# Two-layer streaming-encoder trunk: wide gate and up products and a chunk-row output for S5

## The chip, the cores and the metric

The kernel runs on one core of one Trainium2 chip, in one launch. The metric is the device time of one execution in microseconds, the median of the runs of a kernel. Lower is better.

## The reference, cut to what matters

x has 256 tokens of 1024 features. Each of the two layers computes, in fp32:

```python
h = rms_norm(x, ffn1_pre_g);  x = x + 0.5 * rms_norm(swiglu(h, w_gu, w_down), ffn1_post_g)
h = rms_norm(x, mix_pre_g);   x = x + rms_norm(hybrid_mixer(h, ...), mix_post_g)   # GLA, S5, FoX
h = rms_norm(x, xa_pre_g);    x = x + rms_norm(memory_cross_attention(h, ...), xa_post_g)
h = rms_norm(x, ffn2_pre_g);  x = x + 0.5 * rms_norm(swiglu(h, w_gu, w_down), ffn2_post_g)

def swiglu(h, w_gu, w_down):                      # w_gu 1024 x 5632, w_down 2816 x 1024
    gate, up = jnp.split(h @ w_gu, 2, axis=-1)
    return (jax.nn.silu(gate) * up) @ w_down
```

Inside the mixer, S5 is a grouped complex diagonal state-space model: y = Re(C x_t) + D u with x_t = A x_(t-1) + B u_t, then gelu(y), then y * sigmoid(y @ glu_w + b), then an up projection. The 256 tokens are worked as 64 chunks of 4 tokens.

## The kernel before, in words

**Products in three passes.** Every large operand is split into two fp32r parts: `split` (L232) casts it on ScalarE (`h`, L237) and subtracts on VectorE (`lo`, L241). `mm3` (L253) then issues three matmuls into one accumulator (L255): h·xh, h·xl, lo·xh. The activations x, transposed, stand in two tiles, `xth` (high) and `xtl` (low), 128 x 8 x 256 each, made by `xt` (L273).

**Weights.** `make_plan` lists all weights in the order in which they are used, in pieces of 128 x 1024. SP loads them into `wf` (5 buffers), `split_next` (L162) splits them into a ring `wh`, `wl` of 7 buffers. `take` and `free` walk the ring; `ahead` (L181), called by `tick` (L221) and at the end of `proj_cols`, splits on until six pieces are outstanding. Each split is a ScalarE cast and a VectorE subtraction, in program order with everything else on those engines.

**FFN.** 22 tiles j of 128 hidden features. `proj_cols` (L279) computes one tile: for 8 row blocks kk and for i = 0 (gate) and 1 (up) it calls `mm3` with 128 x 128 weights and 256 moving columns, 48 matmuls into one PSUM bank (tag `mm`, 4 buffers): columns 0 to 255 gate, 256 to 511 up. `act` (L573) makes `sil` on ScalarE (L575) and `h` on VectorE (L577) from that bank, and `split_h` splits h into `hh`, `hl`. Tiles 0 and 1 come from `head`, in another order, out of the boundary between the stages. From j = 4 on, after every even j, `rows_step` (L356) multiplies two finished h tiles by the down weights (24 matmuls with 512 columns into the four `pa` banks, two ticks). After j = 20 that is a single row. `tail` (L365) takes the last five h tiles, 17 to 21, at the end of the stage, token half by token half, with tile 21 as the fifth of each group of five.

**Tasks.** Small work is written as generators; `run_tasks` (L202) advances each by one step, and a `yield n` waits n calls. It is called once in the middle of `proj_cols`, once after each tile, and once per down row, so two calls in an odd tile and four in an even one. The first FFN of each layer starts `s5_setup` (L610) at j = 3; its yields add up to 30 calls, so it ends in tile 13. The setup transposes through `mm` banks (L733) and ends with the powers `er`, `ei` (VectorE, L626).

**S5 (L918)** is such a task in the mixer, interleaved with the gate projections. Its output y is built in bank `py` (pbank(2)): eight matmuls with `m1` (L943) and sixteen with `m3` (L966) as the 128 x 128 stationary operand and 64 moving columns (chunks). They are in plain fp32, and the trace shows two instructions for each. After the gelu steps, `yu` has (position in chunk, channel) on the partitions. It is stored to DRAM (`yd`, L979) and loaded back as `yv` in four pieces (L982), with channels on the partitions; after `yield 5` the GLU product (L988) reads `yv`. SP issues these five transfers in its one queue, between weight loads.

**FoX and GLA** already write outputs of 64 stationary columns to the two partition halves of a bank in turn (L1073, L859, L885).

Of the kernel before, what the change touches and what calls it, by code (L numbers as in the profile page):

```python
# [8 lines left out]
F32 = mybir.dt.float32  # L9
F32R = mybir.dt.float32r  # L10
# [3 lines left out]
ALU = mybir.AluOpType  # L14
AX = mybir.AxisListType
# [3 lines left out]
KT = D // 128  # L19
# [35 lines left out]
class Trunk:  # L55
# [23 lines left out]
    def make_plan(self, depth):  # L79
# [20 lines left out]

        for l in range(depth):
            ffn(l, 1)
            for q in range(2):
                add(a["w_gvr"][l, q])
# [31 lines left out]
            for n in ("xa_k", "xa_q", "xa_v", "xa_o"):  # L136
                for q in range(4):
                    add(a[n][l, q])
            self.parts.append(len(self.plan))
            ffn(l, 2)  # L140
        self.n_dma = self.n_split = self.n_take = self.n_free = self.n_ring = 0
        self.raw, self.ready, self.homes = {}, {}, {}
# [127 lines left out]
    def pbank(self, i):  # L270
        return self.pa.tile([128, 512], F32, tag=f"pa{i}", name="pa")

    def xt(self):  # L273
        h = self.per.tile([128, KT, 256], F32R, tag="xth", name="xth")
        lo = self.per.tile([128, KT, 256], F32R, tag="xtl", name="xtl")
        return h, lo


    def proj_cols(self, xt):  # L279
        xh, xl = xt  # L280
        ps = self.bank()
        for n in range(2):
            h, lo = self.take()
            for k in range(4):
                kk = 4 * n + k
                for i in range(2):
                    w = slice(k * 256 + i * 128, k * 256 + i * 128 + 128)
                    self.mm3(ps[:, i * 256:(i + 1) * 256], (h[:, w], lo[:, w]), (xh[:, kk, :], xl[:, kk, :]),
                             kk == 0 and i == 0, kk == KT - 1 and i == 1)
            self.free()  # L290
            if n == 0:
                self.tick()
        if not self.eager:
            self.ahead()
        return ps


    def proj_rows(self, xt):
        xh, xl = xt
        ps = [self.bank(), self.bank()]  # L300
        for n in range(4):
            h, lo = self.take()
            for k in range(2):
                kk = 2 * n + k
                c = slice(k * 512, (k + 1) * 512)
                for t in range(2):
                    tk = slice(t * 128, (t + 1) * 128)
                    self.mm3(ps[t], (xh[:, kk, tk], xl[:, kk, tk]), (h[:, c], lo[:, c]), kk == 0, kk == KT - 1)
            self.free()
            if n < 3:  # L310
                self.tick()
        self.ahead()
        return ps
# [3 lines left out]
    def head(self, width):  # L317
        w = [self.take() for _ in range(4)]
        ps = [self.bank(), self.bank()]
        kc = HALF // width  # L320


        def go(t, xt, *hooks):
            tk = slice(t * 128, (t + 1) * 128)
            c = 0
            for g in range(2):

                order = ((0, 0), (0, 1), (1, 0), (0, 2), (1, 2), (1, 1)) if g == 0 else (
                    (0, 0), (1, 0), (0, 1), (1, 1), (0, 2), (1, 2))
                for m, (i, n) in enumerate(order):  # L330
                    a, b = PASSES[n]
                    for k in range(kc):
                        kk = ((2 * g + i) * kc + k) % KT
                        out = ps[t] if width == 512 else ps[g][:, t * 256:(t + 1) * 256]
                        first = m == 0 and k == 0 and (g == 0 or width == 256)
                        last = m == 5 and k == kc - 1 and (g == 1 or width == 256)
                        for at, hook in hooks:
                            if c == at:
                                hook()
                        c += width // 256  # L340
                        self.nc.tensor.matmul(out, lhsT=xt[b][:, kk, tk], rhs=w[2 * g + i][a][:, k * width:(k + 1) * width],  # L341
                                              start=first, stop=last)

        return ps, go
# [212 lines left out]
    def ffn(self, xt, ps, pool, extra=None):  # L557
        nc = self.nc
        hs = [None] * NFT

        def two_halves():
            t = pool.tile([128, 2, HALF], F32R, tag="e0", name="we")
            return t[:, 0], t[:, 1]

        self.house((two_halves, lambda: [pool.tile([128, HALF], F32R, tag=n, name="we") for n in ("e1", "e2")]))

        def split_h(j, src):
            hh = pool.tile([128, 256], F32R, tag="hh", name="hh", bufs=6)
            hl = pool.tile([128, 256], F32R, tag="hl", name="hl", bufs=6)
            self.split(hh, hl, src)  # L570
            hs[j] = (hh, hl)

        def act(gate, up, n):  # L573
            sil = pool.tile([128, n], F32, tag=f"sil{n}", name="sil", bufs=2)
            nc.scalar.activation(sil, gate, AF.Silu)  # L575
            h = pool.tile([128, n], F32, tag=f"h{n}", name="h", bufs=2)
            nc.vector.tensor_tensor(h, sil, up, op=ALU.mult)  # L577
            return h

        def first_tiles():  # L580
            for j, p in enumerate(ps):
                h = [act(p[:, t * 256:t * 256 + 128], p[:, t * 256 + 128:t * 256 + 256], 128) for t in range(2)]
                yield 2
                pt = self.bank()
                for t in range(2):
                    nc.tensor.transpose(pt[:, t * 128:(t + 1) * 128], h[t], self.ident)
                split_h(j, pt[:, 0:256])

        self.start(first_tiles())
        acc = None  # L590
        q = 0
        for j in range(2, NFT):
            p = self.proj_cols(xt)
            split_h(j, act(p[:, 0:256], p[:, 256:512], 256))
            self.run_tasks()
            if extra is not None and j == 3:
                self.start(extra())
            if j >= 4 and j % 2 == 0:
                if acc is None:
                    acc = self.acc_banks()  # L600
                n = min(2 * q + 2, NFT - TAIL)
                self.rows_step(acc, hs[2 * q:n], 2 * q, NFT)
                q += 1
        return acc, self.tail(acc, hs[n:], n, NFT)
# [313 lines left out]
    def s5(self, l, com):  # L918
        nc, u4 = self.nc, self.u4
        V, S, T = nc.vector, nc.scalar, nc.tensor  # L920
        m1, m2, m3 = self.m1, self.m2, self.m3
        er, ei, rho = (x[:].rearrange("p j c -> p (j c)") for x in (self.er, self.ei, self.rho))

        def tt(o, x, y, op):
            V.tensor_tensor(o, x, y, op=op)
# [7 lines left out]
        w = com.tile([128, 512], F32, tag="w5", name="w5")  # L933
# [4 lines left out]
        tt(z[:, 1], vi, er, ALU.mult)  # L938
        tt(w, vr, ei, ALU.mult)
        tt(z[:, 1], z[:, 1], w, ALU.subtract)  # L940
        py = self.pbank(2)
        for j in range(8):
            T.matmul(py[:, j * 64:(j + 1) * 64], lhsT=m1[:, j].rearrange("p k h -> p (k h)"), rhs=u4[:, j],  # L943
                     start=j == 0, stop=False)
        yield
        for i in range(2):
            V.tensor_tensor_scan(z[:, i], rho, z[:, i], 0.0, op0=ALU.mult, op1=ALU.add)
# [1 line left out]
        xs = self.per.tile([128, 2, 8, 64], F32, tag="m2", name="xs")  # L949
# [11 lines left out]
        tt(w4, z4[1], e4[0], ALU.mult)  # L961
        tt(x4[1], x4[1], w4, ALU.add)
        yield 2
        for j in range(8):
            for i in range(2):
                T.matmul(py[:, j * 64:(j + 1) * 64], lhsT=m3[:, i, j].rearrange("p k h -> p (k h)"), rhs=xs[:, i, j],  # L966
                         start=False, stop=j == 7 and i == 1)
        yu, y2 = z[:, 0], z[:, 1]
        S.activation(y2, py, AF.Square)
        yield  # L970
# [2 lines left out]
        S.activation(w, y2, AF.Tanh, scale=math.sqrt(2.0 / math.pi))  # L973
        yield
        V.scalar_tensor_tensor(yu, w, 1.0, py, op0=ALU.add, op1=ALU.mult)

        yv = com.tile([128, 4, 2, 64], F32, tag="suh", name="yv")
        yd = self.dr.tile([128, 512], F32, tag="yd", name="yd")
        nc.sync.dma_start(yd, yu)  # L979
        yd = yd[:].rearrange("(e g) (r n) -> e r g n", e=4, r=4)  # L980
        for t in range(4):
            nc.sync.dma_start(yv[:, t].rearrange("p q c -> p (q c)"), yd[3 - t])  # L982
        yv = yv[:].rearrange("p t q c -> p q t c")
        yield 5
        pg = self.pbank(2)
        for c in range(2):
            for k in range(2):
                T.matmul(pg[:, c * 256:(c + 1) * 256], lhsT=self.glw[:, k, c * 128:(c + 1) * 128],  # L988
                         rhs=yv[:, k], start=(k == 0), stop=(k == 1))
# [118 lines left out]
    def mixer(self, l, xt, pvr, com):  # L1108
# [62 lines left out]
        for c in (0, 2):  # L1171
# [5 lines left out]
            self.merge2(2, c, gts, fox + (4,), acc)  # L1177
        gts = [self.gates(xt, com) for _ in range(2)] + [self.gates(xt, lp) for _ in range(2)]
        self.finish(s5)
        self.gp, self.gn = self.gain(self.a["mix_post_g"][l]), self.gain(self.a["xa_pre_g"][l])  # L1180
        self.eager = False
# [362 lines left out]
```

## Time and profile before

| what | us |
|---|---|
| median of 3 runs | 1421.88 |
| lowest, highest run | 1420.07, 1422.84 |
| profiled execution, whole | 1420.51 |
| its span, first to last instruction | 1418.7 |
| TensorE matmul busy | 1402.0 (99%) |
| TensorE weight load busy | 1296.2 (91%) |
| VectorE busy | 924.2 (65%) |
| ScalarE busy | 717.2 (51%) |

1.8 us of the profiled execution lie outside its span. Matmuls are pipelined, so the duration that a matmul row shows (284 ns for 256 columns) is longer than its place in the stream; what one costs is the distance from start to start, which is read from long uninterrupted pieces of the chain of work that ended last. The granted TensorE clock was 0.999 of full speed over the span.

### The profile page before, as it was taken

What the parts mean: (1) busy time and instruction counts of PE and PEld (TensorE: products, weight loads), DVE (VectorE), ACT (ScalarE), POOL (GpSimd) and SP (SyncE); (2) the same over time, 40 slices, a digit from 0 to 9 for tenths busy, and PEclk for the clock granted to TensorE, in tenths of its full rate; (3) what the DMA queues carried; (4) which work ended last, traced back from release to release, by engine and by line L of the source; (5) the groups of instructions that cost most, each with busy time, mean ns of one, the idle gap of its engine ahead of it and who ended that gap; (6) DMA issues with size and microseconds to landing.
All of it is one profiled execution on the core that took longest, in us unless ns stands there. A gap on an engine that the chain in (4) does not pass through costs nothing.

```text
span 1418.7 us, 24657 instructions
## 1 busy us (share of the span) xinstructions
PE 1402.0 (99%) x9970; PEld 1296.2 (91%) x9970; DVE 924.2 (65%) x1383; ACT 717.2 (51%) x1151; POOL 60.3 (4%) x58
## 2 busy tenths in 40 slices
PE   9999999999999999999999999999999999999998
PEld 7999989899979889999999999898999898899997
DVE  6796567855586656555577775667756856665553
ACT  5445447354465545444454545464653645454442
POOL 0000000001210000000001000000022000000000
PEclk9999999999999999999999999999999999999999
DMA  7665637446447437555546566373465565365551
GB/s 277 213 197 160 223 121 211 136 157 229 163 166 252 144 110 263 182 182 190 193 157 207 187 202 194 119 235 97 157 228 178 188 213 180 105 227 191 188 185 41
DMA packets 75892, 257.02 MB, mean 181 GB/s; under 512 B 8673, under 2 KB 11777, under 8 KB 75778
## 3 DMA queue, kind: packets, MB, share of 16 engines
q1 hardware_dynamic: 75778, 255.45, 55.2%
q8 instruction: 78, 1.28, 0.4%
q14 instruction: 36, 0.29, 0.1%
HBM read 253.32 MB, written 2.10 MB: 180 GB/s over the span
## 4 chain that ended last, share of the span: by engine, by line
PE 88%; DVE 6%; ACT 3%; issue 2%; DMA 0%; POOL 0%; DVEq 0%; POOLq 0%; ACTq 0%
PE mm L255 57%; PE pa L255 21%; PE mm L341 4%; DVE wl L241 2%; PE mm L434 1%; ACT wh L237 1%; ACT junk L386 1%; DVE acc L1232 1%; PE mm L931 1%; PE pa L966 0%; DVE xtl L1229 0%; DMA wf<-in_xa_k 0%; PE mm L1073 0%; PE pa L1044 0%; PE pa L1062 0%
## 5 line engine op out<-in xcount | busy, mean ns | idle before, releaser
L241 DVE TENSOR_TENSOR wl<-wf,wh 128x1024 fp32r<-128x1024 f32 (+1 forms) x438 | 521.8, 1205 | 262.0 <-ACT wh L237 261.1
L255 PE MATMUL mm<-xth,wh 128*128 128x256 f32 (+1 forms) x2000 | 567.8, 284 | 0.0
L255 PE MATMUL mm<-xth,wl 128*128 128x256 f32 (+1 forms) x2000 | 566.3, 283 | 0.0
L255 PE MATMUL mm<-xtl,wh 128*128 128x256 f32 (+1 forms) x2000 | 565.4, 283 | 0.0
L237 ACT CAST wh<-wf 128x1024 fp32r<-128x1024 f32 (+1 forms) x442 | 446.0, 1029 | 139.9 <-PE mm L255 51.1
L255 PEld LDWEIGHTS mm<-xth,wh 128*128 128x128 f32 (+1 forms) x2000 | 377.4, 189 | 4.3 <-issue 2.4
L255 PEld LDWEIGHTS mm<-xtl,wh 128*128 128x128 f32 (+1 forms) x2000 | 375.5, 188 | 1.7
L255 PEld LDWEIGHTS mm<-xth,wl 128*128 128x128 f32 (+1 forms) x2000 | 376.4, 188 | 0.0
L255 PE MATMUL pa<-wh,hl 128*128 128x512 f32 x320 | 125.3, 392 | 0.0
L255 PE MATMUL pa<-wl,hh 128*128 128x512 f32 x320 | 125.2, 391 | 0.0
L255 PE MATMUL pa<-wh,hh 128*128 128x512 f32 x320 | 124.8, 390 | 0.0
L575 ACT ACTIVATE sil<-mm 128x256 f32<-128x256 f32 (+1 forms) x96 | 35.1, 366 | 106.9 <-PE mm L255 98.5
L237 ACT CAST hh<-h 128x256 fp32r<-128x256 f32 x80 | 32.5, 406 | 105.3 <-DVE h L577 105.3
L577 DVE TENSOR_TENSOR h<-sil,mm 128x256 f32<-128x256 f32 (+1 forms) x96 | 38.1, 396 | 55.7 <-ACT sil L575 55.7
L255 PEld LDWEIGHTS pa<-wh,hl 128*128 128x128 f32 x320 | 60.0, 188 | 12.7
L255 PEld LDWEIGHTS pa<-wh,hh 128*128 128x128 f32 x320 | 60.2, 188 | 11.6
L255 PEld LDWEIGHTS pa<-wl,hh 128*128 128x128 f32 x320 | 60.1, 188 | 11.8
L393 POOL TENSOR_TENSOR rr<-rv,mhalf 128x1 f32<-128x1 f32 x36 | 23.5, 652 | 953.6 <-DVE rv L392 953.6
L241 DVE TENSOR_TENSOR hl<-h,hh 128x256 fp32r<-128x256 f32 x80 | 34.1, 426 | 37.8 <-ACT hh L237 37.8
L237 ACT CAST xth<-mm 128x512 fp32r<-128x512 f32 x39 | 22.7, 587 | 53.0 <-PE mm L434 22.9
L255 PE MATMUL mm<-mt,wh 128*128 128x256 f32 x256 | 46.5, 284 | 0.0
L1187 ACT ACTIVATE gt<-mm 128x512 f32<-128x512 f32 x24 | 14.3, 596 | 60.6 <-PE mm L255 53.9
(287 smaller groups left out, 1736.5 us busy)
## 6 DMA issues: line engine op xcount, KB each, us to landing
wf<-in_ffn_gu SPq DMA_DIRECT2D x176, 512.0 KB, 4.3
wf<-in_ffn_dn SPq DMA_DIRECT2D x88, 512.0 KB, 4.4
wf<-in_w_cols SPq DMA_DIRECT2D x72, 512.0 KB, 5.0
wf<-in_w_mix SPq DMA_DIRECT2D x16, 512.0 KB, 3.9
wf<-in_xa_k SPq DMA_DIRECT2D x16, 512.0 KB, 6.4
wf<-in_xa_q SPq DMA_DIRECT2D x16, 512.0 KB, 5.8
wf<-in_xa_v SPq DMA_DIRECT2D x16, 512.0 KB, 5.2
wf<-in_xa_o SPq DMA_DIRECT2D x16, 512.0 KB, 3.9
```

The lines of the kernel that those rows point to most:

```text
L237: self.nc.scalar.copy(h, src)
L241: (eng or self.nc.vector).tensor_tensor(full(lo), src, h.bitcast(F32), op=ALU.subtract)
L255: self.nc.tensor.matmul(out, lhsT=lhs[i], rhs=rhs[j], start=start and n == 0, stop=stop and n == 2)
L341: self.nc.tensor.matmul(out, lhsT=xt[b][:, kk, tk], rhs=w[2 * g + i][a][:, k * width:(k + 1) * width], start=first, stop=last)
L386: self.nc.scalar.activation(jk, src, AF.Square, scale=math.sqrt(f / D), accum_out=s)
L393: self.nc.gpsimd.tensor_tensor(r, v, self.mhalf[:, 0:1], op=ALU.pow)
L434: self.nc.tensor.transpose(ps[:, i * 128:(i + 1) * 128], hn[:, k * 128:(k + 1) * 128], self.ident)
L575: nc.scalar.activation(sil, gate, AF.Silu)
L577: nc.vector.tensor_tensor(h, sil, up, op=ALU.mult)
L931: T.matmul(v[:, j * 64:(j + 1) * 64], lhsT=m2[:, i, j], rhs=u4[:, j], start=j == 0, stop=j == 7)
L1187: self.nc.scalar.activation(gt, ps, AF.Tanh, scale=0.5)
L1232: V.tensor_tensor(acc[:, c], acc[:, c], gt, op=ALU.add)
```

## The change

`xt` makes one tile that holds both halves side by side, and keeps a view `both` of 512 columns (high, then low). A new `proj_wide` multiplies the high weight part by all 512 columns in one matmul and the low part by the 256 high columns in a second, and it uses one bank for gate and one for up. The two halves of a bank are added by a VectorE reduction into `gu` in SBUF, from which `act` reads. The FFN uses it from j = 4 on, when `s5_setup` is not running: that is tiles 14 to 21 in the first FFN of a layer and 4 to 21 in the second, 52 tiles in all.

In S5 the operands change places: `u4` and `xs` (64 columns, the chunks) become stationary and `m1`, `m3` (128 columns) move; odd and even j go to different partition halves of `py`. `yu` then has chunks on the partitions, and four transposes into PSUM and one ScalarE copy make `yv`, in place of the store to DRAM and the four loads.

```diff
     def xt(self):
-        h = self.per.tile([128, KT, 256], F32R, tag="xth", name="xth")
-        lo = self.per.tile([128, KT, 256], F32R, tag="xtl", name="xtl")
-        return h, lo
+        x = self.per.tile([128, KT, 2, 256], F32R, tag="xt", name="xt")
+        self.both = x[:].rearrange("p k a b -> p k (a b)")
+        return x[:, :, 0], x[:, :, 1]
...
+    def proj_wide(self, xt):
+        xh, both = xt[0], self.both
+        ps = [self.bank(), self.bank()]
+        for n in range(2):
+            h, lo = self.take()
+            for k in range(4):
+                kk = 4 * n + k
+                for i in range(2):
+                    w = slice(k * 256 + i * 128, k * 256 + i * 128 + 128)
+                    ops = [(ps[i], h[:, w], both[:, kk]), (ps[i][:, 0:256], lo[:, w], xh[:, kk])]
+                    for m, (out, lhs, rhs) in enumerate(ops if kk == 0 else ops[::-1]):
+                        self.nc.tensor.matmul(out, lhsT=lhs, rhs=rhs, start=kk == 0 and m == 0, stop=kk == KT - 1 and m == 1)
+            self.free()
+            if n == 0:
+                self.tick()
+        if not self.eager:
+            self.ahead()
+        return ps
...
+        setup = None
         for j in range(2, NFT):
-            p = self.proj_cols(xt)
-            split_h(j, act(p[:, 0:256], p[:, 256:512], 256))
+            if j > 3 and setup not in self.tasks:
+                p = self.proj_wide(xt)
+                gu = pool.tile([128, 2, 256], F32, tag="gu", name="gu", bufs=2)
+                for i in range(2):
+                    nc.vector.tensor_reduce(gu[:, i], p[i][:].rearrange("p (a c) -> p c a", a=2), axis=AX.X, op=ALU.add)
+                split_h(j, act(gu[:, 0], gu[:, 1], 256))
+            else:
+                p = self.proj_cols(xt)
+                split_h(j, act(p[:, 0:256], p[:, 256:512], 256))
             self.run_tasks()
             if extra is not None and j == 3:
-                self.start(extra())
+                setup = self.start(extra())
...
         py = self.pbank(2)
+        def out(j):
+            return py[64 * (j % 2):64 * (j % 2) + 64].rearrange("p (k j h) -> p k j h", k=4, j=4)[:, :, j // 2]
         for j in range(8):
-            T.matmul(py[:, j * 64:(j + 1) * 64], lhsT=m1[:, j].rearrange("p k h -> p (k h)"), rhs=u4[:, j],
-                     start=j == 0, stop=False)
+            T.matmul(out(j), lhsT=u4[:, j], rhs=m1[:, j], start=j < 2, stop=False)
...
-        for j in range(8):
-            for i in range(2):
-                T.matmul(py[:, j * 64:(j + 1) * 64], lhsT=m3[:, i, j].rearrange("p k h -> p (k h)"), rhs=xs[:, i, j],
-                         start=False, stop=j == 7 and i == 1)
+        for i in range(2):
+            for j in range(8):
+                T.matmul(out(j), lhsT=xs[:, i, j], rhs=m3[:, i, j], start=False,
+                         stop=j > 5 and i == 1)
...
         V.scalar_tensor_tensor(yu, w, 1.0, py, op0=ALU.add, op1=ALU.mult)
+        yield 2
+        pt = self.pbank(2)
+        for k in range(4):
+            T.transpose(pt[:, (3 - k) * 128:(4 - k) * 128], yu[:, k * 128:(k + 1) * 128], self.ident)
         yv = com.tile([128, 4, 2, 64], F32, tag="suh", name="yv")
-        yd = self.dr.tile([128, 512], F32, tag="yd", name="yd")
-        nc.sync.dma_start(yd, yu)
-        yd = yd[:].rearrange("(e g) (r n) -> e r g n", e=4, r=4)
-        for t in range(4):
-            nc.sync.dma_start(yv[:, t].rearrange("p q c -> p (q c)"), yd[3 - t])
+        S.copy(yv[:].rearrange("p t q c -> p (t q c)"), pt)
         yv = yv[:].rearrange("p t q c -> p q t c")
-        yield 5
+        yield 2
```

## Rows read from the trace of the kernel before

**Rows 1.** The page: busy time of the engines, the granted clock in 40 slices, and the chain that ended last by engine and by line.

```profile
PE 1402.0 (99%) x9970; PEld 1296.2 (91%) x9970; DVE 924.2 (65%) x1383; ACT 717.2 (51%) x1151; POOL 60.3 (4%) x58
...
PEclk9999999999999999999999999999999999999999
...
PE 88%; DVE 6%; ACT 3%; issue 2%; DMA 0%; POOL 0%; DVEq 0%; POOLq 0%; ACTq 0%
PE mm L255 57%; PE pa L255 21%; PE mm L341 4%; DVE wl L241 2%; PE mm L434 1%; ACT wh L237 1%; ACT junk L386 1%; DVE acc L1232 1%; PE mm L931 1%; PE pa L966 0%; DVE xtl L1229 0%; DMA wf<-in_xa_k 0%; PE mm L1073 0%; PE pa L1044 0%; PE pa L1062 0%
```

**Rows 2.** The same chain in order of time, in the second FFN of layer 0 (start, length, what): two tiles (96 matmuls) and two down rows (24), again and again.

```profile
593.61 11.52 PE mm L255 x96
605.13 5.48 PE pa L255 x24
610.61 11.52 PE mm L255 x96
```

**Rows 3.** Busy time of each engine in one such pair of tiles and in two stretches of the first FFN of layer 0 (length, busy time and count of each engine, clock, DMA share, GB/s).

```profile
610.61:627.61 17.00, 17.00 (x123) 16.02 (x122) 9.05 (x10) 7.69 (x10) 0.00 (x0) 1.00 0.58 186
118.95:135.95 17.00, 17.00 (x123) 16.02 (x122) 14.68 (x46) 6.46 (x9) 0.00 (x0) 1.00 0.46 141
135.95:152.95 17.00, 17.00 (x123) 16.02 (x122) 12.56 (x15) 9.69 (x13) 0.00 (x0) 1.00 0.77 258
```

**Rows 4.** VectorE in order of time in the pair from 610.61 us (start, length, instruction, in brackets the idle time before it and what ended it), with one ScalarE row, the `sil` of that tile.

```profile
611.78 1.23 DVE L241 TENSOR_TENSOR wl<-wf,wh 128x1024 fp32r<-128x1024 f32 x1 [1.49 <-ACT wh L237]
616.47 0.38 ACT L575 ACTIVATE sil<-mm 128x256 f32<-128x256 f32 x1 [1.97 <-PE mm L255]
616.88 0.42 DVE L577 TENSOR_TENSOR h<-sil,mm 128x256 f32<-128x256 f32 x1 [1.13 <-ACT sil L575]
617.78 0.42 DVE L241 TENSOR_TENSOR hl<-h,hh 128x256 fp32r<-128x256 f32 x1 [0.47 <-ACT hh L237]
618.73 1.23 DVE L241 TENSOR_TENSOR wl<-wf,wh 128x1024 fp32r<-128x1024 f32 x1 [0.52 <-ACT wh L237]
620.29 1.23 DVE L241 TENSOR_TENSOR wl<-wf,wh 128x1024 fp32r<-128x1024 f32 x1 [0.34 <-ACT wh L237]
```

**Rows 5.** Groups of VectorE instructions by shape, over the whole span (count, busy us, mean ns of one, idle time before): the one reduction out of PSUM, the dearest operation with 512 elements, and the two operations on h, one with a PSUM operand and one without.

```profile
L1269 DVE TENSOR_REDUCE nm<-pa 128x2 f32<-128x512 f32 x8 | 5.5, 692 | 3.7 <-PE pa L255 3.0
...
L947 DVE TENSOR_TENSOR_SCAN z<-rho,z 128x512 f32<-128x512 f32 x4 | 4.7, 1210 | 0.0
...
L577 DVE TENSOR_TENSOR h<-sil,mm 128x256 f32<-128x256 f32 x80 | 33.5, 419 | 51.9 <-ACT sil L575 51.9
...
L241 DVE TENSOR_TENSOR hl<-h,hh 128x256 fp32r<-128x256 f32 x80 | 34.1, 426 | 37.8 <-ACT hh L237 37.8
```

**Rows 6.** The end of that FFN in order of time: the last gate/up matmul, the first matmul of the tail, the first two of its fifth row (tile 21), and the steps that make tile 21's h.

```profile
698.36 0.28 PE L255 MATMUL mm<-xth,wl 128*128 128x256 f32 x1
698.49 0.39 PE L255 MATMUL pa<-wh,hh 128*128 128x512 f32 x1
...
701.25 0.62 PE L255 MATMUL pa<-we,hh 128*128 128x512 f32 x2
...
698.75 0.39 ACT L575 ACTIVATE sil<-mm 128x256 f32<-128x256 f32 x1 [1.97 <-PE mm L255]
699.16 0.42 DVE L577 TENSOR_TENSOR h<-sil,mm 128x256 f32<-128x256 f32 x1 [1.13 <-ACT sil L575]
...
699.62 0.41 ACT L237 CAST hh<-h 128x256 fp32r<-128x256 f32 x1 [0.49 <-DVE h L577]
```

**Rows 7.** The first FFN of layer 0: two pieces of the chain, and VectorE's h of tiles 13 to 15. Tile 13 is the first half of the first piece, tiles 15 and 16 are the second.

```profile
118.95 11.52 PE mm L255 x96
...
135.95 11.52 PE mm L255 x96
...
132.50 0.41 DVE L577 TENSOR_TENSOR h<-sil,mm 128x256 f32<-128x256 f32 x1
136.62 0.41 DVE L577 TENSOR_TENSOR h<-sil,mm 128x256 f32<-128x256 f32 x1
143.00 0.42 DVE L577 TENSOR_TENSOR h<-sil,mm 128x256 f32<-128x256 f32 x1
```

**Rows 8.** The chain in the mixer of layer 0: GLA's half-wide products (L859, 256 moving columns), S5's (L943, L966), four transposes (L910), FoX's half-wide products (L1073, four instructions with 256 moving columns and four with 128), and FoX's three transposes behind them and elsewhere (L1062).

```profile
258.18 1.01 PE pa L859 x8
259.19 1.93 PE pa L943 x16
...
282.70 3.52 PE pa L966 x32
286.21 0.44 PE pa L910 x4
...
289.51 0.80 PE mm L1073 x8
290.31 0.48 PE pa L1062 x3
...
293.64 0.33 PE pa L1062 x3
```

**Rows 9.** SP's queue in S5's way through DRAM, layer 0.

```profile
296.55 0.33 SPq L979 DMA_DIRECT2D yd<-z  x1
298.82 2.29 SPq L982 DMA_DIRECT2D yv<-yd  x4
```

## Prediction

> **What bounds the kernel now.** I read the page first: TensorE has matmuls in flight for 99% of the span, at full clock in all 40 slices, and 88% of the chain that ended last is its own [rows 1]. L255, the three-pass matmul, holds 78% of the chain alone. So time is won only by a shorter stream of matmuls, or by closing a wait in it, and the other engines count only where they become late. Then the chain in order of time: in the second FFN it repeats two tiles in 11.52 us and two down rows in 5.48 us without a gap [rows 2], 17.00 us a pair, and TensorE is busy for all of it [rows 3]. A 256-column matmul therefore costs 11.52 / 96 = 0.1200 us from start to start, a 512-column one 5.48 / 24 = 0.2283 us. Twice the columns cost less than twice the time. Last I read who is idle meanwhile: VectorE works 9.05 us of a pair, ScalarE 7.69 us.
>
> **Wide products.** A tile streams 16 x (512 + 256) = 12,288 columns, as 48 x 256 does now; the columns don't change. What goes is 16 of 48 matmuls with their weight loads. Each (kk, i) costs 3 x 0.1200 = 0.3600 us now and 0.2283 + 0.1200 = 0.3483 us after: 0.0117 us less, 0.187 us per tile. Tiles: 18 in each second FFN (4 to 21), 8 in each first one (14 to 21, since the setup's 30 calls are used up in tile 13 at two calls per odd tile and four per even one). 2 x 26 = 52 tiles x 0.187 = **9.7 us less**. No row shows a 512 and a 256 alternating. One end is no saving beside a hidden load, 0; the other is that only columns count: the two prices give (0.2283 - 0.1200) / 256 = 0.423 ns per column, 768 columns 0.325 us, and 832 pairs x 0.035 = 29.1 us less. I take the sum of the two prices, because both come from long streams in which a load stands before every matmul, as it will.
>
> By the Trainium skill (TensorE: Matmul & The Clock Gate, Back-to-back issue gap) a warm matmul costs its columns at 2.4 GHz and 2.5 ns. By that the 16 dropped matmuls of 52 tiles would give only 832 x 2.5 ns = 2.1 us. The rows contradict it, since the line through their two prices leaves 11.7 ns for no columns; it is a rival below.
>
> **The reductions.** Each wide tile adds two on VectorE, 512 elements from PSUM to 256 sums. Nearest row: 0.692 us for 512 elements out of PSUM [rows 5]; below, the 0.42 us of an operation with 256 results; above, 1.21 us, the dearest with 512 elements [rows 5]. I take 0.69, for the same operation, source and input size. h then reads SBUF and keeps its 0.42 us, as hl shows, which reads SBUF now [rows 5]. A pair gets 4 x 0.69 = 2.77 us: 9.05 + 2.77 = 11.8 of the new 16.63 us (17.00 - 2 x 0.187). VectorE's idle time is mostly slack, being waits for a tile's end or for a ring slot; what is real latency is 0.47 + 0.52 + 0.34 us per tile [rows 4], 2.66 per pair. 11.8 + 2.7 = 14.5 < 16.63, so TensorE hides the reductions. If that cover goes, see the second rival. ScalarE gains no instruction; `sil` waits 0.7 us longer, and the weight casts behind it, but six pieces of 2.9 us each lie between a split and its use. SP's loads wait for the same subtractions and keep five buffers.
>
> Banks: a wide tile holds two of four, so tile j + 2 waits for the reductions of tile j, one tile (5.57 us) after its end. In the steady state they are through some 1.3 us after it (0.27 us as `sil` in [rows 6], and two reductions, the first begun before the end). The worst place is the first FFN, where the setup makes VectorE late: h of tile 13 starts at 132.50, 7.8 us after its tile's end (118.95 + 5.76), h of 14 6.1 us, h of 15 1.3 us late [rows 7]. Tile 14's reductions would stand behind hl of 13 and two subtractions, at about 136.6 to 137.9; tile 16 wants the banks at 141.5. VectorE works 12.56 us in that pair [rows 3], with two more reduced tiles 15.3 of 16.6, and catches up one tile later. No stall priced; up to 1.5 us for the bound.
>
> Tail: tile 21 ends at 698.48 and its `sil` starts 0.27 us later; the fifth group wants `hh` at 701.25, 2.77 us after the end, and it is there at 700.03 [rows 6]. Wide, the gate bank closes 0.35 us before the end, so the reductions run from -0.08 to 1.2 us, h to 1.54, `hh` to 2.0: 0.8 us to spare, cost nothing.
>
> **The joint tile for x** changes no instruction. Its writers and readers cover the same blocks as before, and the next x tile is written long after the last product with the old one: 0.
>
> **S5.** Now L943 takes 1.93 us (16 instructions) and L966 3.52 (32) per layer [rows 8]. After, the same number, each with 64 stationary and 128 moving columns, alternating between partition halves. FoX does just that: of its eight instructions in 0.80 us, four have 256 columns; GLA's eight with 256 take 1.01 us, 0.126 each; so the other four cost (0.80 - 0.505) / 4 = 0.074 us [rows 8], too little for 128 fp32 columns unless both halves work at once. 16 x 0.074 = 1.18 and 32 x 0.074 = 2.37: 1.90 us less. Against it the four transposes, 0.44 us, and a change of array shape behind L966, 0.15 us (the three transposes behind FoX's products take 0.48, elsewhere 0.33) [rows 8]; L943 already follows half-wide products. Net -1.31 us a layer, **2.6 us less** in all. Bounds: halves that don't overlap, 0.12 us an instruction, 48 x 0.12 + 0.59 - 5.45 = +0.9 a layer, 1.8 us more; perfect overlap at half of a transpose's 0.11 us, 48 x 0.055 + 0.44 - 5.45 = -2.4 a layer, 4.7 less.
>
> The way through DRAM held SP from 296.55 to 301.1 [rows 9], two loads' worth of time, while TensorE ran on: its removal is worth 0. The transposes come two calls after yu, so nothing queued behind them on TensorE waits; the copy adds about 0.6 us to ScalarE, two calls ahead of the GLU product, which itself moves one call earlier. S5's result isn't wanted before the last merge.
>
> **The sum.** -9.7 - 2.6 = -12.3 us. The profiled execution took 1420.5, span plus 1.8 us; it would become 1408.2. The median is 1.4 us above it, inside the spread of the runs (2.8 us, or 0.2%, also about what a measurement of this kernel tells from no change), so I forecast 1421.9 - 12.3 = **1409.6 us**. Its own range, from the bounds above: -9.7 - 4.7 to -8.2 + 1.8, 1407.5 to 1415.5.
>
> **Rivals.**
> 1. *A matmul saves only its 2.5 ns.* Then 0.1200 us would be the cost of 256 columns beside a load, and dropping one matmul buys little: 1421.9 - 2.1 - 2.6 = 1417.2 us. Against it: the 512-column price. For it: no row has the mixture. 10%.
> 2. *VectorE becomes the bound of the wide tiles: slower.* Price: the reduction over two elements a quarter of a bank row apart runs as two passes, 1.38 us. Then a pair needs 9.05 + 5.54 + 2.66 = 17.25 us, 0.25 over today, x 26 = +6.5; tile 21's `hh` comes 0.6 us late, x 4 = +2.4; S5 -2.6: 1428.2 us. It costs from 1.23 us on ((16.63 - 11.71) / 4) and has eaten the FFN's gain at 1.32. For it: all reductions stand on the path from a tile to its banks. Against it: the nearest row, 0.692 us. 6%. The Trainium skill (VectorE: DVE Perf Modes, Rules for kernel authors) calls the reduction the slowest VectorE operation, always at one element per cycle; the row fits one pass at that pace.
> 3. *Only columns count*: 1421.9 - 29.1 - 2.6 = 1390.2 us. For it: S5's products with 64 moving columns take 0.11 us [rows 8], so a weight load may be what 0.1200 us is made of. Against it: the load before a wide product still has only the narrow one to hide behind. 4%.
> 4. *The first FFN stays narrow*, because the setup lasts beyond my count: 16 tiles x 0.187 = 3.0 us less gain, 1412.6; inside the main range. 6%.
>
> **Numbers.** The forecast has 74%. The range 1405 to 1418 takes in the main case, rivals 1 and 4 and what measurement adds; it leaves out 2 and 3, and about as much again for the unforeseen. Faster by over 0.2% (below 1419.1): most of all but rival 2, 0.88. Within: 0.06. Slower: 0.06.
>
> **What would show it.** Right: the chain in the second FFN shows pairs of 11.15 + 5.48 us; reductions of 0.69 us x 104; VectorE near 11.8 us per pair; L943 and L966 near 1.2 and 2.4 us; no TensorE wait for `hh` in the tails. Wrong: a pair near 16.9 or above (rival 1), waits of the gate product for a reduction (rival 2), a pair near 15.9 (rival 3), 256-column products in tiles 14 to 21 of the first FFN (rival 4).

## The result, and the profile after

The kernel after takes 1412.5 us in the median of 4 runs (1411.04 to 1415.34), beside 1420.97 us before on the same chip: ratio 0.9945, 95% interval 0.9934 to 0.9957. Run once more (`after_again` below) it took 1412.52 us, ratio 0.9938 (0.9924 to 0.9952). Each ratio here and below is against runs of the kernel before on the same chip. The forecast of 1409.6 us was 2.9 us too low, inside its range of 1405 to 1418; of the 12.3 us of gain that it added up, 8.5 were measured.

The first profile after is of the run of 1415.34 us, the longest of the four. TensorE is still at the top of the page, and its share of the chain is 86%, where it was 88% [rows 1]:

```profile
PE 1394.2 (99%) x9146; PEld 1250.0 (88%) x9146; DVE 985.9 (70%) x1487; ACT 718.5 (51%) x1153; POOL 60.4 (4%) x58
...
PE 86%; DVE 6%; ACT 3%; issue 2%; DMA 2%; POOL 0%; DVEq 0%; POOLq 0%; SPq 0%; ACTq 0%
```

There are 824 matmuls fewer: 52 tiles x 16 = 832, less the 8 transposes of S5. VectorE works 62 us more. The chain in the second FFN of layer 0 answers to [rows 2] (start, length, what):

```profile
591.56 11.22 PE mm L311 x64
602.78 5.49 PE pa L255 x24
608.27 11.22 PE mm L311 x64
```

Two tiles now take 64 matmuls and 11.22 us where they took 96 and 11.52. The pair is 16.71 us, 0.29 us less; I had expected 0.37. Busy time by engine in that pair, and in one of the first FFN, answers to [rows 3] (length, then PE, PEld, DVE, ACT and POOL, clock, DMA share, GB/s):

```profile
591.56:608.27 16.71, 16.71 (x89) 14.33 (x89) 11.46 (x14) 7.72 (x10) 0.00 (x0) 1.00 0.58 189
...
136.13:152.84 16.71, 16.71 (x89) 14.33 (x89) 13.93 (x19) 8.38 (x13) 0.00 (x0) 1.00 0.64 225
```

VectorE's groups answer to [rows 5] (count | busy us, mean ns of one | idle time before):

```profile
L621 DVE TENSOR_REDUCE gu<-mm 128x256 f32<-128x512 f32 x104 | 66.9, 685 | 5.5 <-PE mm L311 3.5
...
L599 DVE TENSOR_TENSOR h<-sil,gu 128x256 f32<-128x256 f32 x52 | 22.1, 426 | 5.8 <-DVE gu L621 0.5
```

In the mixer of layer 0 the chain answers to [rows 8]: S5's two products (L979 was L943, L1001 was L966), what stands behind each of them, and the new transposes (L1015):

```profile
258.40 0.87 PE pa L979 x16
259.27 3.00 PE mm L255 x12
...
281.00 1.90 PE pa L1001 x32
282.90 0.59 PE pa L941 x4
...
297.51 0.44 PE pa L1015 x4
```

The table sets the stages side by side, each from the first matmul of a stage's head to that of the next (layer 0, then layer 1; the last runs to the end of the span), in us. `later_wide` is the last version built below.

| stage | before | after | after_again | later_wide |
|---|---|---|---|---|
| first FFN | 195.1 | 193.7 | 193.7 | 193.7 |
| mixer, cross-attention | 318.5 | 317.9 | 316.6 | 315.4 |
| second FFN | 189.9 | 187.5 | 187.5 | 187.6 |
| first FFN | 193.1 | 192.2 | 192.2 | 192.0 |
| mixer, cross-attention | 317.2 | 317.7 | 316.4 | 317.5 |
| second FFN | 195.6 | 194.6 | 194.8 | 193.2 |

The FFNs of the two profiles of after agree to 0.2 us. Their mixer stages don't, 316.4 to 317.9 for the same work, and two windows of 5 us at the start of cross-attention say why. In the first profile after (layer 0):

```profile
410.00:415.00 5.00, 2.72 (x15) 2.11 (x14) 2.46 (x6) 2.42 (x8) 0.56 (x1) 0.92 0.22 80
415.00:420.00 5.00, 5.00 (x33) 5.00 (x33) 3.45 (x7) 3.24 (x9) 1.01 (x2) 0.73 0.00 0
```

and in `after_again`:

```profile
410.00:415.00 5.00, 2.47 (x18) 1.99 (x17) 2.46 (x6) 2.42 (x8) 0.55 (x1) 1.00 0.14 56
415.00:420.00 5.00, 5.00 (x44) 5.00 (x44) 3.38 (x7) 3.24 (x9) 1.07 (x2) 1.00 0.01 3
```

TensorE stands still for half of the first window in both. Once, the granted clock then falls for part of the time from 2.4 to 1.2 GHz (1.00 to a mean of 0.73 in the second window) and TensorE gets 33 matmuls done where it gets 44 at full clock. The change doesn't seem to cause it: the idle stretch is there before as well (TensorE works 2.10 us of the 5 from 413 us), and runs of before lie as far apart, 1419.8 us at a mean clock of 0.999 and 1423.0 at 0.997.

### The profile page after: what moved, and what is told of

The parts are those of the page before. It is cut to its first block, busy times and chain, and to the rows that moved or that the text cites. A ratio compares the mean times of both kernels' runs of the same rounds, so it can differ in the third digit from the quotient of the medians.

```text
span 1413.5 us, 23236 instructions
## 1 busy us (share of the span) xinstructions
PE 1394.2 (99%) x9146; PEld 1250.0 (88%) x9146; DVE 985.9 (70%) x1487; ACT 718.5 (51%) x1153; POOL 60.4 (4%) x58
## 4 chain that ended last, share of the span: by engine, by line
PE 86%; DVE 6%; ACT 3%; issue 2%; DMA 2%; POOL 0%; DVEq 0%; POOLq 0%; SPq 0%; ACTq 0%
PE mm L255 36%; PE pa L255 21%; PE mm L311 21%; PE mm L363 3%; DVE wl L241 2%; ACT wh L237 1%; PE mm L456 1%; DMA wf<-in_xa_k 1%; ACT junk L408 1%; DVE acc L1267 1%; PE mm L962 1%; DVE xt L1264 0%; PE pa L1079 0%; DMA wf<-in_ffn_dn 0%; PE mm L1108 0%
## 5 line engine op out<-in xcount | busy, mean ns | idle before, releaser
L255 PE MATMUL mm<-xt,wh 128*128 128x256 f32 (+1 forms) x2336 | 424.9, 284 | 0.0
L255 PEld LDWEIGHTS mm<-xt,wh 128*128 128x128 f32 (+1 forms) x2336 | 359.5, 188 | 4.0 <-issue 2.4
L255 PE MATMUL mm<-xt,wl 128*128 128x256 f32 (+1 forms) x1168 | 329.5, 282 | 0.0
L311 PE MATMUL mm<-xt,wh 128*128 128x512 f32 x832 | 293.0, 394 | 1.3 <-DVE hl L241 1.3
L311 PE MATMUL mm<-xt,wl 128*128 128x256 f32 x832 | 226.3, 282 | 0.0
L255 PEld LDWEIGHTS mm<-xt,wl 128*128 128x128 f32 (+1 forms) x1168 | 219.3, 188 | 0.0
L311 PEld LDWEIGHTS mm<-xt,wh 128*128 128x128 f32 x832 | 154.8, 188 | 34.2 <-DVE hl L241 1.6
L311 PEld LDWEIGHTS mm<-xt,wl 128*128 128x128 f32 x832 | 156.3, 188 | 4.1
L621 DVE TENSOR_REDUCE gu<-mm 128x256 f32<-128x512 f32 x104 | 66.9, 685 | 5.5 <-PE mm L311 3.5
L255 PE MATMUL pa<-wh,xt 128*128 128x512 f32 x192 | 64.8, 398 | 1.2 <-ACT xt L1268 1.2
```

The costliest lines, as they stand in the source:

```text
L255: self.nc.tensor.matmul(out, lhsT=lhs[i], rhs=rhs[j], start=start and n == 0, stop=stop and n == 2)
L311: self.nc.tensor.matmul(out, lhsT=lhs, rhs=rhs, start=kk == 0 and m == 0, stop=kk == KT - 1 and m == 1)
L621: nc.vector.tensor_reduce(gu[:, i], p[i][:].rearrange("p (a c) -> p c a", a=2), axis=AX.X, op=ALU.add)
```

## The experiments

**The parts one by one.** My theory after reading the traces before and after: the wide tiles give 7.8 us, S5 gives 3.5, and the joint x tile takes back what I had priced at nothing. Three kernels, each the kernel before with one part.

`wide_only`: `proj_wide`, its use in the FFN and the joint tile, with the old S5.

> The kernel before with the wide gate and up products and the joint x tile, and with the old S5. Theory A (the parts add up as the two traces show them): 52 wide tiles x 16 pairs x 0.0094 us = 7.8 us gained, 0.46 us lost at the two boundaries from cross-attention to the second FFN (joint tile), and up to 1.6 us lost where the first wide tile of layer 1's second FFN waits for a bank: 5.7 to 7.3 us faster than before, ratio 0.9949 to 0.9960. Rival (the wide products gain little, and the result came from S5): within 2 us of before. Rival (the clock's dips at the start of the two cross-attentions come with the wide products): the dips are in this trace too, and 2.8 us of the gain go with them.

1415.47 us, ratio 0.9959 (0.9947 to 0.9972), 6.4 us faster by the medians and 5.8 by the ratio: theory A. The first rival falls. The second does too: the clock's dips are in this trace, but one is in that of the new S5 alone as well, and neither is in that of `after_again`.

`s5_only`:

> The kernel before with the new S5 alone (products by rows of chunks, transposes in place of the trip through DRAM), and the old narrow products and two x tiles. Theory A (S5 is on the chain that ends the mixer, at the size that the two traces show): 1.75 + 1.70 = 3.45 us faster, ratio 0.9976. My prediction's size: 2.6 us, ratio 0.9982. Rival (another branch of the mixer, or the boundary behind it, takes the time back): under 1 us faster. If the clock's dips at the start of the cross-attentions come with the new S5, they stand in this trace, with 0.9 to 1.9 us lost at each.

1417.95 us, ratio 0.9975 (0.9964 to 0.9986), 3.9 us faster by the medians and 3.6 by the ratio: theory A in the middle, and my 2.6 us (0.9982) not excluded by the time alone. In layer 1, with the clock at full speed in both traces, the mixer stage takes 315.40 us against 317.16, 1.76 us less; my working had 1.31. One such pair can't tell the two apart: layer 0's stage took 318.45 us before and 317.77 in `joint_only` below, with the old S5 and the clock at full speed in both. The rows of the products can: they come to 1.94 us a layer, as set out further down.

`joint_only`:

```diff
-        h = self.per.tile([128, KT, 256], F32R, tag="xth", name="xth")
-        lo = self.per.tile([128, KT, 256], F32R, tag="xtl", name="xtl")
-        return h, lo
+        x = self.per.tile([128, KT, 2, 256], F32R, tag="xt", name="xt")
+        self.both = x[:].rearrange("p k a b -> p k (a b)")
+        return x[:, :, 0], x[:, :, 1]
```

> The kernel before with one tile for both parts of x in place of two, and nothing else. Theory A (the joint tile is let go one pass later): at the two boundaries from cross-attention to the second FFN, ScalarE's first write of the new x waits for the last product of the tail in place of the last but one, some 0.23 us more each, and TensorE then waits 0.23 to 0.24 us for it ahead of the head's first products: 0.46 us slower in all. Rival (as my prediction put it: nothing): the same stretches are as long as before, within 0.05 us.

Its one run took 1420.97 us, beside a median of 1421.87 us before; a time alone can't show 0.46 us. The stretches that the expectation names can, and in them it is theory A to the hundredth. The chain at the boundary from cross-attention to the second FFN (layer 0), before:

```profile
505.40 16.03 PE pa L255 x69
523.01 5.97 PE mm L341 x46
```

and with the joint tile alone:

```profile
505.22 16.03 PE pa L255 x69
521.25 0.44 PE mm L434 x4
521.69 0.71 PE pa L255 x3
522.40 0.02 issue
522.42 0.59 ACT xt L237
523.01 0.04 issue
523.06 5.97 PE mm L341 x46
```

From the first of the 69 to the head it is 17.61 us before and 17.84 here (layer 1: 17.60 and 17.83). The tail is the last part of the output projection, and it multiplies by the old x tile. With two tiles the high one is let go after the tail's last but one matmul, since the last pass reads only `xtl`; the joint one after the last, one matmul of 0.23 us later, and the cast that writes the new x stands on the chain. The kernel after has the same 17.84 us.

**Why a wide pair costs 0.3506 us and not 0.3483.** Three variants of a tile's 32 matmuls.

`grouped`: per weight half all eight wide products in a row, then all eight narrow ones (the other way round in the second half).

> The kernel after with the wide tile's 32 products in four runs: of each half of the weights the eight of 512 columns in a row and the eight of 256 in a row, in place of one of each by turns. The work is the same. Theory A (alternating between the two widths costs what the pair lies over 0.1200 + 0.2283 us): a pair falls from 0.3506 to 0.3483 us, a wide tile from 5.61 to 5.57 us, and the run is 832 x 0.0023 = 1.9 us faster than after. Rival B (the pair costs 0.3506 us in any order): the same as after, 1412.5 us. Rival C (a run of 256s or of 512s is cheaper or dearer for another reason, such as its wait for the low parts of the weights): the tile is over 5.65 us.

`bank_order`:

```diff
-            for k in range(4):
-                kk = 4 * n + k
-                for i in range(2):
+            for i in range(2):
+                for k in range(4):
+                    kk = 4 * n + k
```

> The kernel after with the loop over gate and up outside that over the four 128-row slices of a weight half, so that eight products in a row write one PSUM bank where before each pair went to the other bank. The work is the same. Grouping the widths showed that a 512-column product of the wide tile starts every 232 ns and a 256-column one every 119 ns, while the 512-column products of the down projection, which stay on one bank, start every 227 ns. Theory A (the change of bank costs the 512-column product 4 to 5 ns): a pair falls from 0.3506 to about 0.347 us, a tile from 5.61 to 5.55 us. Rival B (it is the operand or the weights, not the bank): 5.61 us stays.

`other_moving`:

```diff
-                    ops = [(ps[i], h[:, w], both[:, kk]), ...
+                    ops = [(ps[i], h[:, w], h[:, 0:512]), ...
```

> The kernel after in which the 512-column products stream 512 columns of the weight tile through TensorE in place of the joint x tile (so it computes something else); stationary matrix, shape, count and order stay. The down projection's products stream weights past hidden tiles and start every 227 ns, the wide tile's stream x past weights and start every 230 to 232 ns. Theory A (the joint x tile as the streamed operand makes the 3 to 5 ns): a wide tile falls from 5.61 to about 5.55 us. Rival (it is the stationary side, or the alternation of what is loaded): 5.61 us stays.

Two tiles in the second FFN of layer 0, grouped:

```profile
590.52 11.24 PE mm L311 x64
```

one bank at a time:

```profile
591.85 11.21 PE mm L311 x64
```

streaming weights in place of x:

```profile
592.45 11.13 PE mm L311 x64
```

Neither the order of the widths nor the bank matters: `grouped` is at 1412.95 us, ratio 0.9940 (0.9927 to 0.9954), where the kernel after is, and `bank_order` at 1413.92 us in its one run; rival B in both. With another streamed operand the pair falls to 11.13 / 32 = 0.3478 us, next to the 0.3483 that I had predicted (theory A; 5.565 us a tile where 5.55 was expected; the one run took 1411.74 us). So the last 0.003 us hang on what is streamed. What about it costs them stays open: not the number of columns and not the type, which are the same. `other_moving` streams the same 512 columns of the weight tile for every row block, where the joint x tile gives other columns each time, so it can't say whether the tile counts or that its columns change.

**How much room VectorE has.** I had called its idle time "mostly slack".

`double_reduce` runs every reduction twice:

```diff
-                    nc.vector.tensor_reduce(gu[:, i], ...)
+                    for _ in range(2):
+                        nc.vector.tensor_reduce(gu[:, i], ...)
```

> The kernel after with each of the 104 reductions done twice: 104 x 0.685 = 71 us more work for VectorE, nothing else. In the steady part of an FFN VectorE goes from 11.46 to 14.2 us of each 16.71 us pair, and beside S5's set-up in the first FFN from 13.93 to 16.67. Theory A (VectorE has room and is not on the path, as the prediction took it; the banks are let go 1.4 us later, within the time of a tile): pairs stay at 16.71 us, at most 1 us is lost beside S5's set-up and at the starts and ends of the FFNs, ratio to before 0.994 to 0.995. Rival (VectorE, or the bank that waits for it, is already about to become the bound, rival 2 of the prediction): pairs over 17.0 us and the whole 8 us or more slower than after.

1440.44 us, ratio 1.0134 (1.0119 to 1.0150): some 27 us slower than after by the ratios. Theory A is right for the steady pairs, which stay at 16.71 us with 14.04 us of VectorE, and wrong for the FFNs' ends, to which it gave 1 us. The rival has the size, but not the place. The loss is at the ends of the FFNs (against the first profile after the stages grow by 11.6, 6.9 and 10.0 us; the last one, with no head behind it, by none). The waits of TensorE over the whole span (in total, times, longest):

```profile
PE pa L255 <- ACT hh L237: 21.3, 6, 7.1
```

In neither profile of the kernel after is there such a wait. With it the clock falls to 1.2 GHz: TensorE is idle through the 5 us from 195 us, and the granted clock is 0.52 there and 0.50 in the next 5. How the rest divides wasn't followed up.

`half_more` runs one of the two twice (`for i in (0, 1, 1)`).

> The kernel after with one of the two reductions of each wide tile done twice: 52 x 0.685 = 36 us more work for VectorE, half of what the doubled one had. VectorE then has 12.8 us of work in a pair of 16.71 us, where the kernel after has 11.5 and the doubled one 14.0. Theory A (VectorE is still able to catch up between the first wide tile of a first FFN, where it is 6.4 us behind, and the FFN's last tiles, as in the kernel after; the doubled one could not): under 5 us slower than after. Rival (the loss goes with the added work): 13 us slower, half of the doubled kernel's.

1422.53 us, ratio 1.0011 (1.0000 to 1.0022): 10 us slower than `after_again` on the same chip, all of the gain gone. The rival (13 us) is the nearer one, theory A (under 5) is out. The chain at the end of the first FFN of layer 0 shows it:

```profile
183.29 1.21 DVE gu L621 x2
...
184.53 0.70 DVE gu L621
...
188.32 2.35 DVE wl L241 x2
190.67 1.21 DVE gu L621 x2
191.88 0.02 issue
191.90 0.70 DVE gu L621
...
193.16 0.41 ACT hh L237
193.57 0.04 issue
193.62 12.26 PE pa L255 x45
```

The last tile's reductions stand behind weight subtractions that stand behind the last but one tile's reductions. They start 1.6 us after their tile's end, `hh` is ready 4.55 us after it, and the tail waits 1.8 us. Three such waits, at the ends of the first three FFNs, make 6.2 us, and after each of them the granted clock is 0.50 for some 3 us, as it isn't at these places in the kernel after. In the steady state a late reduction costs nothing, because an h tile waits there for its turn in the down projection; at the end nothing is left to wait behind. In the kernel after the same steps in layer 0's second FFN are (start, length, instruction, idle time before; then the tail's fifth row):

```profile
693.71 1.22 DVE L241 TENSOR_TENSOR wl<-wf,wh 128x1024 fp32r<-128x1024 f32 x1
...
694.85 1.28 DVE L621 TENSOR_REDUCE gu<-mm 128x256 f32<-128x512 f32 x2
...
696.69 0.41 ACT L237 CAST hh<-h 128x256 fp32r<-128x256 f32 x1 [0.65 <-DVE h L599]
...
697.34 0.62 PE L255 MATMUL pa<-we,hh 128*128 128x512 f32 x2
```

`hh` is there at 697.10 and wanted at 697.34. The predicted 0.8 us to spare is 0.24, since the reductions begin behind a weight subtraction, not at the bank's closing. At the end of layer 1's first FFN it is 0.05 (`hh` at 888.98, the product at 889.03). The kernel after just fits.

**S5's halves.** `s5_one_side` takes the chunks in the order 0, 2, 4, 6, 1, 3, 5, 7 in both products.

> The kernel after with the order of S5's eight chunks changed from 0, 1, 2 ... 7 to 0, 2, 4, 6, 1, 3, 5, 7 in the two products that write the output bank: neighbours then stand on the same half of TensorE's output side, where they stood on the two halves by turns. The work is the same. Theory A (the products' 1.0 and 1.90 us come from two neighbours on different halves running beside one another): the 32 products of the second go from 1.90 towards the old 3.52 us, the 16 of the first from 1.0 towards 1.93, so up to 2.5 us a layer and 5 us in all slower than after. Rival (the gain comes from the shape, 64 weight columns and 64 moving columns, whichever half they stand on): 1.90 us stays, and the time is that of after within 0.3 us.

Layer 0's chain:

```profile
258.12 1.36 PE pa L979 x16
...
281.21 2.50 PE pa L1001 x32
```

Neither alone. The shape, 64 stationary and 128 moving columns (not 64, as I wrote), takes the second product from 3.52 us [rows 8] to 2.50, the alternation of the halves from there to 1.90. The whole is at 1415.42 us, ratio 0.9962 (0.9948 to 0.9976), some 2 to 3 us slower than after, of which the products explain 2 x (0.49 + 0.60) = 2.2.

**A version without the two losses.** `later_wide` cuts the joint x tile in two along the contraction and starts the second FFN's wide tiles one tile later:

```diff
-        x = self.per.tile([128, KT, 2, 256], F32R, tag="xt", name="xt")
+        x = [self.per.tile([128, 4, 2, 256], F32R, tag=f"xt{n}", name="xt") for n in range(2)]
...
-            if j > 3 and setup not in self.tasks:
+            if j > (3 if extra is not None else 4) and setup not in self.tasks:
```

> The kernel after with two edits that show in different stretches. Edit 1: the joint x tile is cut in two along the contraction (rows 0 to 3 and 4 to 7 of the eight), both parts of x still side by side in each. Theory A (the whole joint tile waits for its last reader): the first write of the new x at the boundary from cross-attention to the second FFN then waits for the third slice of the tail alone, TensorE's 0.24 us wait for it goes, and the stretch falls from 17.84 us to 17.6 or less, 0.4 to 0.5 us in all. Rival: it stays at 17.84 us. Edit 2: the second FFN's first wide tile is the fourth hidden tile after the head's two in place of the third. Theory A (the first wide tile waits for a bank that the head's tiles still hold, 0 to 1.3 us from run to run): no wait of TensorE for the low part of a hidden tile there, at a price of 2 x 0.15 us. Rival: the wait moves on to the next tile. Together 0 to 1.5 us faster than after.

1411.65 us, ratio 0.9934 (0.9922 to 0.9947). The boundary:

```profile
501.45 16.03 PE pa L271 x69
517.48 0.44 PE mm L472 x4
517.92 0.71 PE pa L271 x3
```

In order of time, the tail's last three matmuls, the cast that writes the new x, and the head's first product:

```profile
517.67 0.94 PE L271 MATMUL pa<-we,xt 128*128 128x512 f32 x3
517.96 0.59 ACT L253 CAST xt<-mm 128x512 fp32r<-128x512 f32 x1 [1.93 <-PE mm L472]
...
518.81 1.86 PE L379 MATMUL mm<-wh,xt 128*128 128x256 f32 x12
```

From the first of the 69 to the head that is 17.36 us, 0.48 less than with the whole joint tile and 0.25 less than before the change, because the new x can be written while the tail still reads the other half of the old one. The second edit answers to a wait that the first profile after showed in layer 1. There the chain runs from a late load of weights through ScalarE and VectorE to the bank that the head's tiles still hold:

```profile
1230.36 6.53 DMA wf<-in_ffn_dn
...
1236.97 1.05 ACT wh L237
...
1244.20 1.23 DVE wl L241
1245.42 0.34 DVE hl L241
1245.77 0.04 issue
1245.81 2.71 PE mm L311 x14
```

`after_again` and `later_wide_again` put both on one chip:

> The kernel after once more, beside the next kernel on one chip. Expected 0.9945 of before as the first time. Whether TensorE waits for a bank at the first wide tile of a second FFN (1.3 us in layer 1 in the first profile, nothing in layer 0) is expected to differ from profile to profile, 0 to 1.3 us; the wait of 0.24 us for the new x at both boundaries from cross-attention to the second FFN is expected to be there again.

> The kernel with the joint x tile cut in two and the second FFNs' first wide tile one later, once more, beside the kernel after. Expected from the stages of its first profile: 2 x 0.48 us less at the two boundaries, 2 x 0.15 us more for the two narrow tiles, 0 to 1.3 us less for the bank: 0.7 to 2 us faster than the kernel after. Rival: no difference, in which case the 0.48 us come back later in the second FFN.

After: 1412.52 us (1411.27 to 1414.38), ratio 0.9938 (0.9924 to 0.9952), with a wait of 1.5 us for the bank in layer 1. `later_wide`: 1410.66 us (1409.60 to 1411.07), ratio 0.9921 (0.9908 to 0.9935), without one. The intervals overlap; but every run of it is below every run of after here. The wait for the new x is gone in both of its profiles. So is that for the bank, but this one comes and goes: 1.3 and 1.5 us in the two profiles of after, and 0 to 1.0 us, in one layer or the other, in the seven of other kernels with the same first wide tile (none in two of them). Two profiles without it make it likely that the second edit ends this wait, and don't prove it. It is the fastest version run.

## Why the prediction was right, and where it was not

- **Wide products**: the mechanism holds and the size was off. 52 tiles, as counted. A pair costs 0.3506 us, not 0.3483, so a tile gives 0.15 us and not 0.187: 7.8 us, not 9.7. The sum of the two prices was the right model (`other_moving` gives 0.3478); the 512 price had been read from a stream with another moving operand. Rivals 1 and 3 are out: a tile at 5.61 us, where they needed 5.72 and 5.20. The section of the Trainium skill that the prediction sets beside rival 1 (TensorE: Matmul & The Clock Gate, Back-to-back issue gap) gives the 2.5 ns for an isolated gap, and says that in a stream of weight loads and matmuls both set the spacing. The rows agree with that proviso (0.1200 and 0.2283 us a matmul, a load before each), though not with the 131 ns that the section measured for 512 columns in such a stream; it was wrong to read them as contradicting the Trainium skill on the 2.5 ns.
- **Reductions**: 685 ns, 0.69 predicted, hidden in the steady pairs (11.46 us of VectorE, 11.8 predicted). That TensorE hides them was right for the kernel after, and by less than I argued. I compared VectorE's work and waits with a pair's time and found 2.1 us free, and at the FFN's end 0.8 us. The end is the narrow place, and that step was mis-sized: from -0.08, two reductions of 0.69 end at 1.30 and not at 1.2, and with 0.42 for h and 0.41 for `hh` my own figures leave some 0.6 us; the weight subtraction ahead, which I had left out, takes most of the rest, and 0.24 and 0.05 us were measured. One and a half times the reductions cost 10 us. Rival 2 put its threshold at a reduction of 1.23 us; at 1.03 for each bank (`half_more`) the gain was already gone.
- **Banks**: no stall, as priced, in the first FFN, the place I had called the worst: its first wide tile is reduced 6.4 us late and VectorE has caught up three tiles on. The stall is at the start of the second FFN, which I hadn't looked at: 1.3 and 1.5 us in layer 1 in the two profiles of after, less in the others.
- **The joint tile**: the step "changes no instruction ... 0" failed. The next x tile is written long after the last product with the old one in the FFNs, but not in the output projection of cross-attention, whose tail reads the x tile to its last matmul: 2 x 0.23 us.
- **S5**: 48 instructions a layer at 0.074 us were 3.55 us; they took 0.87 + 1.90 = 2.77 (0.058 each). The transposes at 0.44 us were exact, and so was the 0.15 us for the change of shape behind the second product (0.59 against 0.44). The first product pays it too, which I had left out because it follows half-wide products: 3.00 against 2.85 us behind it. Net 1.06 + 1.62 - 0.30 - 0.44 = 1.94 us of TensorE a layer, 1.76 in the one stage compared, where 1.31 was predicted. By the Trainium skill (TensorEngine Tiling (Array Packing), Key Properties) another tiling mode drains the array, while tiles within one mode run independently. The runs fit both: 0.15 us more at each change, 1.90 us in place of 2.50 when the halves alternate.

Together: -7.8 - 3.5 = -11.3 us from the two mechanisms, where I had -12.3. Given back: 0.5 us by the joint tile and, in the profiles of after, 1.4 by the bank. That leaves -9.4; -8.5 and -9.3 were measured by the medians, -7.8 and -8.8 by the ratios. The clock doesn't explain what is missing: in `before` and `after_again` it was at full speed through all six stages' matmuls, and their sum in the table falls by 8.2 us, with a bank wait of 1.5 us in it. The mixer stage of layer 1 gives 0.8 us there, that of layer 0 1.9. Where about 1 us went stays open.

The forecast stood in its range partly by luck. The wide products fell 1.9 us short and 1.9 us of waits were priced at nothing; S5 gave 0.9 us more than priced, and the median of before beside the result was 0.9 us lower than the one I had started from.

## What to carry to other kernels

A price per instruction holds for the operands it was read from; here another moving operand took 0.0023 of the 0.0117 us that a pair was to save. When two tiles are joined, look for the last reader of each and for who writes next: the whole is let go only with its last part, and cutting along another axis can be better than before. Judge an engine's room at the end of a stage, where each result is wanted at once, and not from its busy share in the steady state.

## What the runs showed of the hardware that was not expected

A 512-column product of the wide tile costs 0.003 us more with the joint x tile as the streamed operand than with the same 512 columns of a weight tile each time (a pair of 0.3506 against 0.3478 us). The order of the widths (0.3513) and of the banks (0.3503) changes little.

In S5's second product, in fp32, an instruction with 64 stationary and 128 moving columns takes 0.078 us when its neighbours stand on the same half of the output partitions (2.50 / 32) and 0.059 us when they alternate between the halves (1.90 / 32); the old shape, 128 stationary and 64 moving, took 0.11 us (3.52 / 32).
